# A hybrid mLSTM and GLA decoder step: three column tiles at the head of the weight stream, in nine small steps, with matmuls of ones ahead of the data

## The chip, the cores and the metric

The kernel runs on one core of one Trainium2 chip. The metric is the device time of one launch in microseconds. Each time below is the median of several runs; beside it stands one profiled execution, from which all rows are taken.

## The reference, cut to what matters

One layer takes 264 rows of activations (256 positions of a prompt, and 8 decode sequences of one position), projects them with one wide weight, runs two recurrent branches, merges them and ends with a LayerNorm:

```
p = x @ w_in                                   # (264, 2048) @ (2048, 13336)
qk_pre, a_v, a_i, a_f, a_o, a_z, b_q, ... = split(p)
qk = silu(causal_conv4(qk_pre))                # the first 2048 columns
...  mLSTM branch, GLA branch, headwise norms, gates ...
ya, yb = ya @ w_pa, yb @ w_pb
y = (sigmoid(g_a) * ya + sigmoid(g_b) * yb) @ w_out
out = layernorm(ALPHA * x + y)
```

All inputs are float32. Every weight is used once, for all 264 rows.

## The kernel before, in words

The kernel is a stream of column tiles ("units", the list of `units()`). A unit is 128 columns of a weight: 16 k tiles of 128 rows each. TensorE holds a weight tile of 128 x 128 and streams the 264 activation columns of one k tile past it. For float32 accuracy each operand is split in two: `hi` is the value rounded by ScalarE to the fast float32r format (`A.copy`), `lo` is the rest, which VectorE subtracts. A k tile then takes three matmuls into the same PSUM bank: hi·x_hi (line 224), hi·x_lo (line 225), lo·x_hi (line 228). A unit is thus 48 matmuls.

Weights come by DMA on SP's queue in pieces of up to 8 k tiles (`load_raw`, a ring of 4 raw buffers), `cast_piece` splits a piece (rings of 5 buffers each for hi and lo), and `group` runs the matmuls of a unit. The order of TensorE's instructions is the order in which the program is written (`manual_schedule`); the other engines' instructions are ordered by priority, casts of weights ahead. Each unit has an epilogue on ScalarE and VectorE; for the first 16 units it is `e_qk`, the convolution and SiLU, which reads the unit's PSUM bank. The pool `ps_m` holds three such banks, `ps_s` five for other work.

The head is special, since x is not in SBUF yet. The first HU = 2 units are loaded in pieces of KH = 4 k tiles, and go through together: for each of four steps the program loads four k tiles of x (line 1120, 528 KiB) and then four k tiles of unit 0 and of unit 1 (line 182, 256 KiB each, side by side in one raw buffer), splits x (lines 210 and 211), splits each unit's piece (lines 204 and 205), and runs the 12 matmuls of unit 0 and of unit 1 on these k tiles. After the four steps the unit loop (from line 1132) starts with the epilogues of units 0 and 1 and the stream of unit 2.

The parameters `par` and `cst`, which the convolution needs, are loaded behind the head's loads (lines 1130 and 1131).

Of the kernel before, what the change touches and what calls it, by code (L numbers as in the profile page):

```python
# [13 lines left out]
F32 = mybir.dt.float32  # L14
F32R = mybir.dt.float32r
# [8 lines left out]
T = L + NB  # L24
KT = 16
# [7 lines left out]
SMALL = 48  # L33
# [10 lines left out]
KR = 8  # L44
# [1 line left out]
CAST_BUFS = 5  # L46
NC = KT // KR
LA = CAST_BUFS - NC
HU = 2
KH = 4  # L50

COL = {}
_off = 0
# [28 lines left out]


@with_exitstack
def body(ctx, tc, xT, wbig, wsmall, par, cmask, lmask, rowc, gate, wgu, cT, sT, nst, cst, lnr,
         y, yd, pC, pn, pm, pconv, pS, sC, sn, sm, sS):
    nc = tc.nc
    V, A, G, PE = nc.vector, nc.scalar, nc.gpsimd, nc.tensor
    const = ctx.enter_context(tc.tile_pool(name="const", bufs=1))
    wraw_p = ctx.enter_context(tc.tile_pool(name="wraw", bufs=RAW_BUFS))  # L90
    whi_p = ctx.enter_context(tc.tile_pool(name="whi", bufs=CAST_BUFS))
    wlo_p = ctx.enter_context(tc.tile_pool(name="wlo", bufs=CAST_BUFS))
# [4 lines left out]
    ps_m = ctx.enter_context(tc.tile_pool(name="ps_m", bufs=3, space=PSUM))  # L97
    ps_s = ctx.enter_context(tc.tile_pool(name="ps_s", bufs=5, space=PSUM))
    UN = units()

    def t4(shape, name, dt=F32):
        return b4.tile(shape, dt, tag="b4", name=name)
# [37 lines left out]
    ones = const.tile([128, 128], F32, name="ones")  # L140
# [10 lines left out]
    x_hi = [const.tile([128, 4, T], F32R, name=f"xh{i}") for i in range(4)]  # L151
    x_lo = [const.tile([128, 4, T], F32R, name=f"xl{i}") for i in range(4)]
# [2 lines left out]
        return ap.bitcast(F32)  # L155


    pieces = [(u, k, KH, u) for k in range(0, KT, KH) for u in range(HU)]
    idx = HU
    for n, (kind, j) in enumerate(UN):  # L160
        if n < HU:
            continue
# [3 lines left out]
    last = {n: i for i, (n, k, w, bi) in enumerate(pieces)}  # L166
    raws, his, los = {}, {}, {}
    nxt = {"dma": 0, "cast": 0}

    def load_raw():  # L170

        i = nxt["dma"]
        if i >= len(pieces):
            return
        r = wraw_p.tile([128, KR, 128], F32, tag="raw", name="raw")
        o = 0
        while i < len(pieces) and o + pieces[i][2] <= KR:
            n, k, m, bi = pieces[i]
            w = 128 if bi is not None else SMALL
            src = wbig[bi] if bi is not None else wsmall  # L180
            raws[i] = r[:, o:o + m, 0:w]
            nc.sync.dma_start(out=raws[i], in_=src[:, k:k + m, :])
            o += m
            i += 1
        nxt["dma"] = i

    def cast_piece():
        i = nxt["cast"]
        while nxt["dma"] <= i:
            load_raw()  # L190
        n, k, m, bi = pieces[i]
        nxt["cast"] += 1
        r = raws.pop(i)
        h = whi_p.tile([128, KR, 128], F32R, tag="hi", name="hi")[:, 0:m]
        if bi is None:
            w = SMALL
            A.copy(out=h[:, :, 0:w], in_=r)
            V.tensor_tensor(out=h[:, :, w:2 * w], in0=r, in1=f(h[:, :, 0:w]), op=ALU.subtract)
            for q in range(m):
                his[n, k + q] = h[:, q, 0:2 * w]  # L200
            return
        lo = wlo_p.tile([128, KR, 128], F32R, tag="lo", name="lo")[:, 0:m]
        with tc.high_priority(offset=PRIO):
            A.copy(out=h, in_=r)  # L204
            V.tensor_tensor(out=lo, in0=r, in1=f(h), op=ALU.subtract)  # L205
        for q in range(m):
            his[n, k + q], los[n, k + q] = h[:, q], lo[:, q]

    def split(hi, lo, src):
        A.copy(out=hi, in_=src)  # L210
        V.tensor_tensor(out=lo, in0=src, in1=f(hi), op=ALU.subtract)

    def parts(n, k0, k1, rhs, base=0):

        small = UN[n][0] == "small"
        m = 2 * SMALL if small else 128
        ps = ps_m.tile([128, 512], F32, tag="mm", name="mm")
        out = ps[0:m, 0:T]
        for k in range(k0, k1):
            if k % KH == 0:  # L220
                yield ps[:, 0:T]
            wh = his[n, k]
            rh, rl = rhs(k - base)
            PE.matmul(out, lhsT=wh, rhs=rh, start=(k == k0), stop=False)  # L224
            PE.matmul(out, lhsT=wh, rhs=rl, start=False, stop=small and k == k1 - 1)  # L225
            if small:
                continue
            PE.matmul(out, lhsT=los[n, k], rhs=rh, start=False, stop=(k == k1 - 1))  # L228

    def group(*a, **kw):  # L230
        for ps in parts(*a, **kw):
            pass
        return ps

    def x_rhs(k):
        return x_hi[k // 4][:, k % 4, :], x_lo[k // 4][:, k % 4, :]
# [873 lines left out]

    with tc.manual_schedule(engines=MANUAL):
        V.memset(ones, 1.0)
        V.memset(inv256, 1.0 / 256.0)
        V.memset(eps_c, EPS)
        V.memset(one_c, 1.0)
        first = [parts(u, 0, 16, x_rhs) for u in range(HU)]
        head = {}
        for i in range(4):
            xr = t4([128, 4, T], "xr")
            nc.sync.dma_start(out=xr, in_=xT[:, 4 * i:4 * i + 4, :])  # L1120
            while nxt["dma"] < HU * (i + 1):
                load_raw()
            split(x_hi[i], x_lo[i], xr)
            for u in range(HU):
                cast_piece()
                head[u] = next(first[u])
        for u in range(HU):
            for _ in first[u]:
                pass
        nc.sync.dma_start(out=par_sb, in_=par)  # L1130
        nc.sync.dma_start(out=cst_sb, in_=cst)
        for n, (kind, j) in enumerate(UN):
            st['n'] = n
            while nxt["cast"] < min(last[n] + 1 + LA, len(pieces)):
                cast_piece()
                while nxt["dma"] < min(nxt["cast"] + RAW_BUFS - 1, len(pieces)):
                    load_raw()
            if kind == "pab":
                pa = group(n, 0, 8, lambda k: (st["yah"].t(k), st["yal"].t(k)))
                pb = group(n, 8, 16, lambda k: (st["ybh"].t(k), st["ybl"].t(k)), base=8)  # L1140
                e_pab(pa, pb, j)
            elif kind == "out":
                ln_pre(j)
                if j >= 8:
                    ln_shift(j)
                ps = group(n, 0, 16, lambda k: (mh.t(k), ml.t(k)))
                e_out(ps, j)
            else:
                ps = head[n] if n in head else group(n, 0, 16, x_rhs)
                if n == 0:  # L1150
                    g_conv_prep()
                if n == 4:
                    V.tensor_copy(out=im_sb, in_=ident)
                    for dst, src in ((gate_sb, gate), (wgu_sb, wgu), (rc_sb, rowc), (cm_sb, cmask), (lm_sb, lmask)):
                        nc.sync.dma_start(out=dst, in_=src)
                if kind == "qk":
                    for _ in e_qk(ps, j):
                        pass
                elif kind == "small":
                    add(g_gates(ps), True)  # L1160
                elif kind == "av":
                    e_v(ps, j, "avt", "avd")
                elif kind == "bv":
                    e_v(ps, j, "bvt", "bvd")
                elif kind == "bq":
                    e_plain(ps, j, "gq", Q_SCALE)
                elif kind == "bk":
                    e_plain(ps, j, "gk")
                elif kind in ("ao", "az"):
                    e_raw(ps, 2 * j + (kind == "az"), "ozr", 4, g_oz)  # L1170
                elif kind == "bz":
                    e_raw(ps, j, "bzr", 4, g_bz)
                elif kind in ("ga", "gb"):
                    e_raw(ps, 2 * j + (kind == "gb"), "gr", 4, g_g)
            pump(BUDGET)
            if kind == "gb" and j == 15:
                drain()
        ln_final()
# [18 lines left out]
def _layout(v):  # L1197
# [5 lines left out]
    d = {}  # L1203
# [1 line left out]
    d["xT"] = np.ascontiguousarray(x.T.reshape(16, 128, T).transpose(1, 0, 2))  # L1205
    w_in, w_pa, w_pb, w_out = v["w_in"][0], v["w_pa"][0], v["w_pb"][0], v["w_out"][0]
    un = units()
    big = np.empty((len(un) - 1, 128, 16, 128), w_in.dtype)
    i = 0
    for kind, j in un:  # L1210
        if kind == "small":
            continue
        if kind == "pab":
            c = slice(j * 128, j * 128 + 128)
            big[i, :, 0:8] = w_pa[:, c].reshape(8, 128, 128).transpose(1, 0, 2)
            big[i, :, 8:16] = w_pb[:, c].reshape(8, 128, 128).transpose(1, 0, 2)
        else:
            src, c0 = (w_out, j * 128) if kind == "out" else (w_in, COL[kind] + j * 128)
            big[i] = src[:, c0:c0 + 128].reshape(16, 128, 128).transpose(1, 0, 2)
        i += 1  # L1220
# [11 lines left out]
    lnr = np.zeros((128, D), np.float32)  # L1232
# [11 lines left out]
    for l in range(5):  # L1244
        hs = 1 << l
        j = np.arange(64)[None, :]
# [65 lines left out]
```

## Time and profile before

| | |
|---|---|
| time, median of 3 runs | 833.69 us (833.45 to 833.74) |
| the profiled execution, its own time | 835.32 us |
| its span, first to last instruction | 833.2 us |
| TensorE busy | 817.1 us, 98% of the span |
| VectorE, ScalarE busy | 593.2 us (71%), 444.8 us (53%) |
| DMA, mean over the span | 224 GB/s |
| mean granted TensorE clock | 0.997 |

Busy time of TensorE counts each matmul from its start to a modelled end, so that consecutive ones overlap; its idle time is more telling than its busy time. The time of an execution is some 2 us above its span, and the medians are read against each other.

### The profile page before, as it was taken

How to read it: one execution, taken by the hardware profiler on the slowest of the kernel's cores; microseconds unless marked ns; L12 is line 12 of the kernel's file. 1: busy time of each engine (PE TensorE's matmuls, PEld its weight loads, DVE VectorE, ACT ScalarE, POOL GpSimd, SP SyncE). 2: the span in 40 equal slices, each digit the busy share in tenths (PEclk: the TensorE clock that was granted, in tenths of full speed). 3: DMA queues.
4: the chain of work that ended last, by engine and by line, in shares of the span. 5: the costliest groups of instructions: out<-in, count | busy, mean ns of one | idle time of the engine just before them, and what ended most of it. 6: DMA issues, size and time to landing. Idle time of an engine off the chain costs nothing.

```text
span 833.2 us, 16677 instructions
## 1 busy us (share of the span) xinstructions
PE 817.1 (98%) x6750; PEld 807.6 (97%) x6750; DVE 593.2 (71%) x971; ACT 444.8 (53%) x669; POOL 44.4 (5%) x75
## 2 busy tenths in 40 slices
PE   6999999999999999999999999999999999999996
PEld 6999999999999999999999999999999999999995
DVE  6877667645567688867667997798746767667962
ACT  5755457545554465455546766566544444444633
POOL 0000000000000000001000000012000000000311
PEclk9999999999999999999999999999999999999998
DMA  8765564857658885688778588987555555576613
GB/s 323 249 199 182 152 205 155 234 181 253 236 185 303 299 298 197 214 281 296 262 253 313 192 284 330 301 277 230 187 183 184 184 179 179 181 252 203 188 39 105
DMA packets 55797, 186.30 MB, mean 224 GB/s; under 512 B 8340, under 2 KB 9304, under 8 KB 55720
## 3 DMA queue, kind: packets, MB, share of 16 engines
q1 hardware_dynamic: 51592, 170.82, 62.6%
q0 software_dynamic: 4128, 14.42, 4.5%
q8 instruction: 53, 0.87, 0.4%
q14 instruction: 24, 0.20, 0.1%
HBM read 168.50 MB, written 16.71 MB: 222 GB/s over the span
## 4 chain that ended last, share of the span: by engine, by line
PE 94%; DVE 2%; DMA 2%; issue 1%; ACT 0%; ACTq 0%; SPq 0%; POOLq 0%; POOL 0%; DVEq 0%
PE mm L224 29%; PE mm L225 29%; PE mm L228 29%; DMA gak<-rows_d 1%; DVE lo L205 1%; PE sd L464 1%; PE sd L702 1%; DMA raw<-wbig 1%; PE sd L423 1%; PE sd L404 0%; PE sd L438 0%; PE sd L753 0%; PE sd L996 0%; PE sd L312 0%; PE sd L964 0%
## 5 line engine op out<-in xcount | busy, mean ns | idle before, releaser
L224 PE MATMUL mm<-xh,hi 128*128 128x264 f32 x1552 | 445.9, 288 | 7.4 <-ACT hi L204 7.4
L225 PE MATMUL mm<-xl,hi 128*128 128x264 f32 x1552 | 440.1, 284 | 0.0
L228 PE MATMUL mm<-xh,lo 128*128 128x264 f32 x1536 | 435.9, 284 | 0.0
L204 ACT CAST hi<-raw 128x1024 fp32r<-128x1024 f32 (+1 forms) x260 | 268.1, 1034 | 274.1 <-PE mm L225 224.5
L205 DVE TENSOR_TENSOR lo<-raw,hi 128x1024 fp32r<-128x1024 f32 (+1 forms) x260 | 314.7, 1214 | 111.4 <-ACT hi L204 107.2
L224 PEld LDWEIGHTS mm<-xh,hi 128*128 128x128 f32 x1552 | 292.9, 189 | 9.0 <-ACT hi L204 7.4
L225 PEld LDWEIGHTS mm<-xl,hi 128*128 128x128 f32 x1552 | 293.1, 189 | 0.2
L228 PEld LDWEIGHTS mm<-xh,lo 128*128 128x128 f32 x1536 | 288.9, 188 | 0.2 <-DVE lo L205 0.2
L225 PE MATMUL mm<-ml,hi 128*128 128x264 f32 x256 | 72.9, 285 | 0.0
L224 PE MATMUL mm<-mh,hi 128*128 128x264 f32 x256 | 72.8, 285 | 0.0
L228 PE MATMUL mm<-mh,lo 128*128 128x264 f32 x256 | 72.5, 283 | 0.0
L566 DVE SCALAR_TENSOR_TENSOR cch<-kq,avd,cch 128x256 f32<-128x256 f32 x64 | 29.1, 480 | 37.0 <-DMA kq<-kq_d 37.0
L224 PEld LDWEIGHTS mm<-mh,hi 128*128 128x128 f32 x256 | 48.2, 188 | 0.0
L228 PEld LDWEIGHTS mm<-mh,lo 128*128 128x128 f32 x256 | 48.1, 188 | 0.0
L225 PEld LDWEIGHTS mm<-ml,hi 128*128 128x128 f32 x256 | 48.0, 188 | 0.0
L551 ACT ACTIVATE cch<-cch,decb 128x512 f32<-128x512 f32 x32 | 21.6, 718 | 39.4 <-DMA cch<-cT 39.4
L225 PE MATMUL mm<-ybl,hi 128*128 128x264 f32 x128 | 36.4, 284 | 0.0
L224 PE MATMUL mm<-ybh,hi 128*128 128x264 f32 x128 | 36.4, 284 | 0.0
L225 PE MATMUL mm<-yal,hi 128*128 128x264 f32 x128 | 36.3, 284 | 0.0
L228 PE MATMUL mm<-yah,lo 128*128 128x264 f32 x128 | 36.3, 284 | 0.0
L224 PE MATMUL mm<-yah,hi 128*128 128x264 f32 x128 | 36.2, 283 | 0.0
L228 PE MATMUL mm<-ybh,lo 128*128 128x264 f32 x128 | 36.2, 283 | 0.0
(314 smaller groups left out, 806.2 us busy)
## 6 DMA issues: line engine op xcount, KB each, us to landing
raw<-wbig SPq DMA_DIRECT2D x252, 512.0 KB, 4.8
cch<-cT SPq DMA_DIRECT2D x16, 512.0 KB, 6.9
kq<-kq_d SPq DMA_DIRECT2D x16, 512.0 KB, 8.2
sC<-cch POOLq DMA_DIRECT2D x16, 512.0 KB, 5.3
sch<-sT SPq DMA_DIRECT2D x8, 512.0 KB, 8.5
gak<-rows_d SPq DMA_DIRECT2D x8, 512.0 KB, 7.6
sS<-sch POOLq DMA_DIRECT2D x8, 512.0 KB, 6.0
xr<-xT SPq DMA_DIRECT2D x4, 528.0 KB, 6.6
```

The lines of the kernel that those rows point to most:

```text
L204: A.copy(out=h, in_=r)
L205: V.tensor_tensor(out=lo, in0=r, in1=f(h), op=ALU.subtract)
L224: PE.matmul(out, lhsT=wh, rhs=rh, start=(k == k0), stop=False)
L225: PE.matmul(out, lhsT=wh, rhs=rl, start=False, stop=small and k == k1 - 1)
L228: PE.matmul(out, lhsT=los[n, k], rhs=rh, start=False, stop=(k == k1 - 1))
L423: PE.matmul(S[:, o:o + n], lhsT=kT.t(2 * h + d)[:, s0:s0 + 128], rhs=qT.t(2 * h + d)[:, t0:t0 + n], start=(d == 0), stop=(d == 1))
L464: PE.matmul(CN[:, 0:VC], lhsT=kw[:, s, d * 128:d * 128 + 128], rhs=vt[h // 2][:, s, h % 2, :], start=(s == 0), stop=(s == 1))
L551: A.activation(out=chunks[i][:, b], in_=chunks[i][:, b], func=AF.Copy, scale=decb[:, h, b0 + b:b0 + b + 1])
L566: V.scalar_tensor_tensor(out=c[:, b, e], in0=r[:, 0, b], scalar=avd[:, j, b0 + b:b0 + b + 1], in1=c[:, b, e], op0=ALU.mult, op1=ALU.add)
L702: PE.matmul(pl[s0:s0 + m, 4 * hf + h, n0:n0 + w].rearrange("p (n s) -> p n s", s=hs), lhsT=K[:, h, hf * 128 + s0:hf * 128 + s0 + m], rhs=r ...
```

## The change

The head takes three units (HU = 3) instead of two, and nine steps of 1, 1, 2, 2, 2, 2, 2, 2 and 2 k tiles instead of four steps of 4. A step has one load of x (132 KiB for each k tile) and one load of the weights of all three units (192 KiB for each k tile) from a new input `whead`, in which the three units' columns stand side by side by k tile. It splits x in one pair of instructions and the weights of all units in one pair, without the raised priority of `cast_piece`, and then runs its matmuls, unit by unit. Unit 0's sums are in a bank of `ps_s`, those of units 1 and 2 in banks of `ps_m`. Ahead of the first step, TensorE runs eight float32 matmuls of the `ones` tile by itself, 128 columns each, into a further bank of `ps_s`, whose content nobody reads.

The raw, hi and lo buffers of the head come from the same rings as before, one of each for a step, of which 3 or 6 of 8 tiles are used. The stream then goes on with unit 3. `wbig` no longer holds the first three units; what is loaded, and the number of matmuls on data, stay the same in total.

```
-HU = 2
-KH = 4
+HU = 3
+HEAD = (1, 1, 2, 2, 2, 2, 2, 2, 2)
...
-    pieces = [(u, k, KH, u) for k in range(0, KT, KH) for u in range(HU)]
-    idx = HU
+    pieces = []
+    idx = 0
...
+    def products(out, n, k, rhs, start, stop, base=0):
 
         small = UN[n][0] == "small"
+        wh = his[n, k]
+        rh, rl = rhs(k - base)
+        PE.matmul(out, lhsT=wh, rhs=rh, start=start, stop=False)
+        PE.matmul(out, lhsT=wh, rhs=rl, start=False, stop=small and stop)
+        if not small:
+            PE.matmul(out, lhsT=los[n, k], rhs=rh, start=False, stop=stop)
...
         V.memset(ones, 1.0)
+        warm = side_ps()
+        head = [(side_ps() if u == 0 else ps_m.tile([128, 512], F32, tag="mm", name="mm"))[:, 0:T] for u in range(HU)]
...
-        first = [parts(u, 0, 16, x_rhs) for u in range(HU)]
-        head = {}
-        for i in range(4):
-            xr = t4([128, 4, T], "xr")
-            nc.sync.dma_start(out=xr, in_=xT[:, 4 * i:4 * i + 4, :])
-            while nxt["dma"] < HU * (i + 1):
-                load_raw()
-            split(x_hi[i], x_lo[i], xr)
+        for _ in range(8):
+            PE.matmul(warm[:, 0:128], lhsT=ones, rhs=ones, start=True, stop=True)
+        k0 = 0
+        for m in HEAD:
+            k1, i, o = k0 + m, k0 // 4, k0 % 4
+            xr = t4([128, m, T], "xr")
+            nc.sync.dma_start(out=xr, in_=xT[:, k0:k1, :])
+            wr, wh, wl = (p.tile([128, KR, 128], dt, tag=t, name=t)[:, 0:HU * m].rearrange("p (k u) c -> p k u c", u=HU)
+                          for p, dt, t in ((wraw_p, F32, "raw"), (whi_p, F32R, "hi"), (wlo_p, F32R, "lo")))
+            nc.sync.dma_start(out=wr, in_=whead[:, k0:k1])
+            split(x_hi[i][:, o:o + m], x_lo[i][:, o:o + m], xr)
+            split(wh, wl, wr)
             for u in range(HU):
-                cast_piece()
-                head[u] = next(first[u])
-        for u in range(HU):
-            for _ in first[u]:
-                pass
+                for k in range(k0, k1):
+                    his[u, k], los[u, k] = wh[:, k - k0, u], wl[:, k - k0, u]
+                    products(head[u], u, k, x_rhs, k == 0, k == KT - 1)
+            k0 = k1
...
-            while nxt["cast"] < min(last[n] + 1 + LA, len(pieces)):
+            while nxt["cast"] < min(last.get(n, -1) + 1 + LA, len(pieces)):
...
-                ps = head[n] if n in head else group(n, 0, 16, x_rhs)
+                ps = head[n] if n < HU else group(n, 0, 16, x_rhs)
```

`parts` and the old `group` become `products` and a `group` without the pauses at every fourth k tile.

## Rows read from the trace of the kernel before

**Rows 1.** The profile page, part 1: busy time and share of the engines.

```profile
PE 817.1 (98%) x6750; PEld 807.6 (97%) x6750; DVE 593.2 (71%) x971; ACT 444.8 (53%) x669; POOL 44.4 (5%) x75
```

**Rows 2.** Waits of TensorE, whole span: total us, times, longest.

```profile
PE mm L224 <- ACT hi L204: 7.4, 1, 7.4
PE sd L702 <- DVE gq L709: 1.0, 1, 1.0
PE sd L642 <- DVE ns L635: 0.5, 1, 0.5
```

**Rows 3.** Timeline from 0 us, all engines: start, length, instruction, idle before.

```profile
0.84 0.17 DVE L1112 MEMSET ones<- 128x128 f32 x1 [0.84 <-PEq L1301]
...
4.41 1.07 ACT L210 CAST xh<-xr 128x1056 fp32r<-128x1056 f32 x1 [2.39 <-DMA xr<-xT]
...
6.71 1.29 ACT L204 CAST hi<-raw 128x512 fp32r<-128x512 f32 x2 [1.22 <-DMA raw<-wbig]
...
7.38 0.59 PE L224 MATMUL mm<-xh,hi 128*128 128x264 f32 x1 [7.38 <-ACT hi L204]
...
8.70 1.07 ACT L210 CAST xh<-xr 128x1056 fp32r<-128x1056 f32 x1 [0.70 <-DMA xr<-xT]
...
11.80 0.42 PE L224 MATMUL mm<-xh,hi 128*128 128x264 f32 x1
...
12.02 0.35 PE L225 MATMUL mm<-xl,hi 128*128 128x264 f32 x1
...
12.20 0.28 PE L228 MATMUL mm<-xh,lo 128*128 128x264 f32 x1
```

**Rows 4.** Busy time by stretch; (x) counts starts; last columns clock, DMA share, GB/s.

```profile
0.00:3.23 3.23, 0.00 (x0) 0.00 (x0) 0.32 (x4) 1.28 (x1) 0.20 (x4) 1.00 0.41 101
0.00:3.78 3.78, 0.00 (x0) 0.00 (x0) 0.32 (x4) 1.28 (x1) 0.20 (x4) 1.00 0.49 145
...
4.00:6.50 2.50, 0.00 (x0) 0.00 (x0) 0.98 (x1) 1.07 (x1) 0.00 (x0) 1.00 0.92 232
6.50:12.00 5.50, 4.62 (x19) 4.39 (x20) 3.83 (x6) 3.96 (x6) 0.00 (x0) 1.00 1.03 400
0.00:12.20 12.20, 4.82 (x20) 4.59 (x21) 5.33 (x10) 6.52 (x8) 0.20 (x4) 1.00 0.84 285
...
12.20:112.20 100.00, 100.00 (x829) 99.94 (x828) 76.82 (x135) 55.52 (x92) 0.72 (x1) 1.00 0.66 216
```

**Rows 5.** Timeline of SP's queue, 0 to 12 us.

```profile
1.19 0.90 SPq L182 DMA_DIRECT2D raw<-wbig  x2
...
10.04 0.33 SPq L1131 DMA_DIRECT2D cst_sb<-cst  x1
11.46 0.33 SPq L182 DMA_DIRECT2D raw<-wbig  x1
```

**Rows 6.** Groups by line and shape, 0 to 45 us: busy us, mean ns.

```profile
L205 DVE TENSOR_TENSOR lo<-raw,hi 128x1024 fp32r<-128x1024 f32 x12 | 14.6, 1221 | 1.2 <-ACT hi L204 1.2
L204 ACT CAST hi<-raw 128x1024 fp32r<-128x1024 f32 x13 | 13.4, 1048 | 5.7 <-PE mm L225 2.7 <-DVE lo L205 1.6 <-DMA raw<-wbig 1.5
L205 DVE TENSOR_TENSOR lo<-raw,hi 128x512 fp32r<-128x512 f32 x8 | 5.2, 686 | 0.6 <-ACT hi L204 0.6
...
L204 ACT CAST hi<-raw 128x512 fp32r<-128x512 f32 x8 | 4.6, 616 | 1.3 <-DMA raw<-wbig 1.2
...
L261 DVE SCALAR_TENSOR_TENSOR cacc<-mm,par_sb,cacc 128x254 f32<-128x254 f32 x5 | 2.4, 481 | 0.0
...
L248 DVE TENSOR_TENSOR dtap<-dtap,ct 128x128 f32<-128x128 f32 x2 | 0.6, 288 | 0.0
```

**Rows 7.** The chain that ended last, 185 to 190 us: eight plain float32 matmuls.

```profile
186.19 1.74 PE sd L464 x8
```

**Rows 8.** Stretches behind the last matmul, columns as in rows 4.

```profile
825.94:827.90 1.96, 0.00 (x0) 0.00 (x0) 0.20 (x1) 1.25 (x3) 0.33 (x1) 1.00 1.04 291
827.90:829.00 1.10, 0.00 (x0) 0.00 (x0) 0.00 (x0) 0.00 (x0) 0.53 (x2) 0.51 1.08 333
```

More of the change, by code (lines that the diff above doesn't have):

```diff
@@ L84, in body @@
 @with_exitstack
-def body(ctx, tc, xT, wbig, wsmall, par, cmask, lmask, rowc, gate, wgu, cT, sT, nst, cst, lnr,
+def body(ctx, tc, xT, whead, wbig, wsmall, par, cmask, lmask, rowc, gate, wgu, cT, sT, nst, cst, lnr,
          y, yd, pC, pn, pm, pconv, pS, sC, sn, sm, sS):
@@ L211, in split, with group @@
         V.tensor_tensor(out=lo, in0=src, in1=f(hi), op=ALU.subtract)
-    def parts(n, k0, k1, rhs, base=0):
+    def products(out, n, k, rhs, start, stop, base=0):
         small = UN[n][0] == "small"
-        m = 2 * SMALL if small else 128
+        wh = his[n, k]
[4 more added lines that the diff above has]
+            PE.matmul(out, lhsT=los[n, k], rhs=rh, start=False, stop=stop)
+    def group(n, k0, k1, rhs, base=0):
         ps = ps_m.tile([128, 512], F32, tag="mm", name="mm")
-        out = ps[0:m, 0:T]
+        out = ps[0:2 * SMALL if UN[n][0] == "small" else 128, 0:T]
         for k in range(k0, k1):
[L220 to L231, printed above, removed]
-            pass
-        return ps
+            products(out, n, k, rhs, k == k0, k == k1 - 1, base)
+        return ps[:, 0:T]
     def x_rhs(k):
@@ L1115, in body @@
         V.memset(one_c, 1.0)
-        first = [parts(u, 0, 16, x_rhs) for u in range(HU)]
-        head = {}
-        for i in range(4):
-            xr = t4([128, 4, T], "xr")
-            nc.sync.dma_start(out=xr, in_=xT[:, 4 * i:4 * i + 4, :])
-            while nxt["dma"] < HU * (i + 1):
-                load_raw()
-            split(x_hi[i], x_lo[i], xr)
-            for u in range(HU):
-                cast_piece()
-                head[u] = next(first[u])
-        for u in range(HU):
-            for _ in first[u]:
-                pass
+        for _ in range(8):
[10 more added lines that the diff above has]
+            split(wh, wl, wr)
+            for u in range(HU):
+                for k in range(k0, k1):
+                    his[u, k], los[u, k] = wh[:, k - k0, u], wl[:, k - k0, u]
+                    products(head[u], u, k, x_rhs, k == 0, k == KT - 1)
+            k0 = k1
         nc.sync.dma_start(out=par_sb, in_=par)
@@ L1207, in _layout @@
     un = units()
-    big = np.empty((len(un) - 1, 128, 16, 128), w_in.dtype)
+    big = np.empty((len(un) - 1 - HU, 128, 16, 128), w_in.dtype)
+    d["whead"] = np.ascontiguousarray(w_in[:, COL["qk"]:COL["qk"] + HU * 128].reshape(16, 128, HU, 128).transpose(1, 0, 2, 3))
     i = 0
-    for kind, j in un:
+    for kind, j in un[HU:]:
         if kind == "small":
@@ L1302 @@
     args = []
-    for name in ("xT", "wbig", "wsmall", "par", "cmask", "lmask", "rowc", "gate", "wgu", "cT", "sT", "nst", "cst", "lnr"):
+    for name in ("xT", "whead", "wbig", "wsmall", "par", "cmask", "lmask", "rowc", "gate", "wgu", "cT", "sT", "nst", "cst", "lnr"):
         a = arrays[name]
```

## The prediction, made before the changed kernel ran

> **What bounds the kernel now.** I read the busy shares first. TensorE works 817.1 of the 833.2 us [rows 1], so 16.1 us of the span hold no matmul. The waits of TensorE say where they are: 7.4 us before the first matmul, and 1.5 us in two waits in the middle [rows 2]. The other 7.3 us lie behind the last matmul at 825.94 us [rows 8]; the change does not touch them. Between the first and the last matmul TensorE is the bound: 829 matmuls start in the 100 us from 12.20 us, 0.1206 us apart [rows 4]. A head that reaches this pace earlier moves everything behind it forward by as much, unless a new wait takes it back.
>
> The timeline of the start shows two losses. The first matmul is at 7.38 us, released by a cast which had waited for the first weights until 6.71 us [rows 3]. And the first matmuls are slow: those at 11.80 and 12.02 us still stand 0.22 us apart, and from 12.20 us the pace is 0.1206 us [rows 3, 4]. For 264 columns these are the clock's two levels, 1.2 and 2.4 GHz; the window view's clock column says 1.00 in both stretches, so here I trust the distances. The clock rose about 4.7 us after the first matmul, and by 12.20 us 20 matmuls had started [rows 4]. So I ask one thing of the change: when does its 21st matmul on data start, with the full pace behind it? Before, that was 12.20 us.
>
> **Landing times.** All head loads are in one queue, so I treat them as a line of KiB. x's first load (528 KiB) is seen at 4.41 us, the first weights (784 KiB in all) at 6.71 us [rows 3]. SP's 14th load goes out at 10.04 us and its 15th at 11.46 us, with its queue idle before them [rows 5]; these fit the landings of the sixth (2080 KiB) and the seventh (2608 KiB), and I read this as eight loads in flight. From 784 KiB at 6.71 us to 2608 KiB at 11.40 us the line is 389 KiB/us, and it gives 10.04 us for 2080 KiB, just what the row shows, and 8.73 us for the fourth load (1568 KiB), seen at 8.70 [rows 3]. Early on it is slower: 256 KiB took the 2.3 us from 4.41 to 6.71, and the DMA engines, though 92% busy, moved 232 GB/s, against 400 from 6.5 us on [rows 4].
>
> Now the new loads: 324 KiB a k tile, 132 of x and 192 of weights.
> - Step 0 (324 KiB in all): by 3.23 us the engines had moved 101 GB/s x 3.23 us = 326 kB, or 319 KiB; by 3.78 us 535 KiB, and 528 KiB were seen at 4.41, some 0.6 us later [rows 4, 3]. So step 0 lands at 3.9 us.
> - Step 1 (648 KiB): between 4.41 and 6.71 us by its share, 120 of 256 KiB: 5.5 us.
> - Step 2 (1296 KiB): 6.71 + 512 / 389 = 8.0 us. Each later step of two k tiles is 648 / 389 = 1.67 us later.
>
> **The splits.** From 512 and 1024 columns, ScalarE's cast is 0.18 us + 0.84 ns a column, VectorE's subtraction 0.15 us + 1.05 ns a column [rows 6]. A step of two k tiles has 768 columns of weights (0.83 and 0.95 us) and 528 of x (0.63 and 0.70); a step of one has 384 (0.51 and 0.55) and 264 (0.41 and 0.43). Hand-overs take some 0.05 us [rows 3].
>
> **The new head on TensorE.** Step 0: weights at 3.9, cast to 4.4, first matmul at 4.46; the lo part is there at 5.0, and the nine matmuls at 0.22 us end at 6.6. Step 1: landed 5.5, lo part ready at 6.6, nine matmuls to 8.6. Step 2: landed 8.0, cast to 8.9, its hi matmuls (19th and 20th) from 8.95; VectorE ends the lo part at 9.9, and the 21st matmul starts at 9.97 us. The clock: 4.7 us after a first matmul at 4.46 is 9.2 us, in time. From there a step is 18 matmuls, 18 x 0.1206 = 2.17 us, against 1.67 of loads, 1.46 of ScalarE and 1.65 of VectorE: TensorE is the slowest and the lead grows. The tightest is step 3: landed 9.7, lo part 11.6, wanted at 9.97 + 16 x 0.1206 = 11.9.
>
> The sum: 12.20 - 9.97 = 2.2 us earlier. The profiled execution would be 835.32 - 2.2 = 833.1 us, and the median of the runs, 1.6 us below that execution, 833.69 - 2.2 = 831.5 us.
>
> **The rest of the change, at nothing.** The eight matmuls of ones wait only for the memset (0.84 us, first on VectorE [rows 3]). Eight float32 matmuls of 257 columns take 1.74 us at the high clock [rows 7], so 0.11 us for 128 columns, about 0.2 us at the low one: 1.1 to 2.7 us, covered by the wait for step 0. At worst, if fewer columns save nothing, they end at 1.1 + 8 x 0.44 = 4.6 us, 0.15 us into step 0, which has slack. Whether they raise the clock the rows cannot show: if they count, it rises from about 1.1 + 4.7 = 5.8 us on, which gives nothing as long as step 2's weights bind.
>
> SP: 18 loads at about 0.45 us each [rows 5]; step 2's weights are the sixth, out by 3.1 us. With eight in flight the ninth waits for the first (about 3.2 us), the tenth also for raw buffer 0, free when step 0's lo part is done, 5.0 us; four steps are queued by then. `par` and `cst` move behind the 18th load and land at 6.71 + (5547 - 784) / 389 = 19.0 us; the first reader that matters is unit 0's epilogue at about 23.5 us. Unit 3's first piece lands 1.3 us behind them and is split by 22.6 us; TensorE wants it at 9.97 + 124 x 0.1206 = 24.9 us. That is 2.3 us of cover; beyond it each us costs one. Moving unit 2 into the head adds no matmul.
>
> **What the pages say.** By the Trainium skill, "DMA: Bandwidth & Descriptors" (Rules for kernel authors; Bandwidth), loads should be batched to 1 MiB or more, and its table has 138 GB/s for 64 KB against 341 for 1 MB. This speaks against loads of 132 KiB: at 138 GB/s, as an estimate from that page, the 648 KiB of the first two steps alone would take 4.8 us behind the first issue. The rows here disagree in part: loads of 256 and 528 KiB together ran at 400 GB/s once eight were in flight [rows 4].
>
> **Rivals.**
> - *Loads go by count, not by KiB.* Every load is 128 rows, and in the slow stretch the engines were 92% busy at half the bytes [rows 4], as if a row had a price of its own. By count, step 0's weights (second load) land at 6.71 us, step 1's (fourth) at 8.70, step 2's (sixth) at 10.04 [rows 3, 5]; the 21st matmul is at 11.98 us and 0.2 us are gained: 833.5. Then the change does not do what it says: its first matmul comes hardly earlier. Against it: the same short rows of weights fit the 389 KiB/us from 6.71 us on. In between lies 832.5.
> - *The slow stretch was its own.* If 389 KiB/us hold from 4.41 us, step 2 lands at 6.4 us. Then TensorE's own low-clock pace binds (steps 0 and 1 end at 8.6), the 21st is at 9.0, a gain of 3.2 us; if the matmuls of ones also raise the clock, step 2's lo part binds at 8.3, a gain of 3.9 us: 829.8.
> - *The clock stays low: slower than before.* Pieces that arrive one by one leave TensorE idle between steps. Each us at 1.2 GHz behind 9.97 us costs 1 - 0.1206 / 0.22 = 0.45 us. The gain is gone if the clock rises only at 9.97 + 2.2 / 0.45 = 14.9 us; later than that the kernel is slower, at 18.6 us by 1.7 us: 835.4. For it: after the last matmul the clock fell to 0.51 after 1.96 us of idle time [rows 8], and the pause between the ones and step 0 is about 1.8 us. Against it: my steps 0 and 1 run nearly without a gap, and in the kernel before a lone start was enough. The Trainium skill, "TensorE: Matmul & The Clock Gate" (Why this matters for your kernels), also wants sustained activity before the clock rises, and calls loops that wait for a DMA between matmuls cold; the rows agree in that the clock rose late and fell with idle time [rows 4, 8].
> - *Given back behind the head.* Three epilogues fall due at once. Unit 4 reuses unit 1's bank at 24.9 + 5.8 = 30.7 us. VectorE has by then, from 20 us, three splits (3.7 us), the preparation (seven instructions like that of line 248, 2.0 us) and two epilogues of some 2.0 us (three like that of line 261, two shorter): 29.7 us [rows 6]. If two more splits come first, TensorE waits 1.3 us and the gain is 0.9: 832.8.
>
> **How the numbers follow.** 0.2% (1.7 us) is about what a measurement of this kernel can tell from no change. Landing by KiB with the clock in time has 0.5; its own range is 830.9 to 832.3, and a fifth of it falls short of 832.0. Loads by count, or halfway there, 0.2; the quick start 0.12; the late clock 0.1, of which 0.04 slower by over 0.2%; given back 0.08, of which 0.03 slower. Faster: 0.4 + 0.12 = 0.52; slower 0.07; the rest, 0.41, within 0.2%. The range goes from the quick start to loads by count, 829.9 to 833.5.
>
> **What would show it.** The first matmul on data at about 4.5 us, the 21st at about 10.0, distances of 0.12 us from there, and unit 3 from about 24.9 us without a wait. Step 2's cast should begin at 8.0 us, released by its DMA. A cast at 10 us means loads by count; distances of 0.22 us after 10 us mean the clock. A wait of TensorE between 24 and 40 us means the gain was given back. The prediction is wrong if the middle of the stream shows new waits, for I took it to move as one piece.

## The result, and the profile after

The changed kernel took 841.69 us (median of 4, 840.76 to 844.2) against 833.72 us for the kernel before: ratio 1.0095, interval 1.0073 to 1.0117. It is 8 us slower, where 2.2 us faster was forecast. The profiled execution is the slowest of the four (844.2 us, span 842.4 us).

In this profile the head came out nearly as predicted. The timeline of TensorE, from the start, and ScalarE's cast of step 2's weights:

```profile
1.06 3.78 PE L1115 MATMUL sd<-ones 128*128 128x128 f32 x16 [1.06 <-DVE ones L1108]
4.49 0.57 PE L218 MATMUL sd<-xh,hi 128*128 128x264 f32 x1
...
8.93 0.28 PE L219 MATMUL sd<-xl,hi 128*128 128x264 f32 x1
9.70 0.39 PE L221 MATMUL sd<-xh,lo 128*128 128x264 f32 x1 [0.49 <-DVE lo L211]
```

```profile
7.82 0.83 ACT L210 CAST hi<-raw 128x768 fp32r<-128x768 f32 x1 [0.33 <-DMA raw<-whead]
```

The first matmul on data is at 4.49 us (predicted 4.46), the 21st at 9.70 (predicted 9.97), the distances behind it are 0.12 us, and unit 3 begins at 24.88 us (predicted 24.9; 27.23 before). Up to here the change gains 2.35 us. Then come the waits of TensorE over the whole span (total, times, longest), which answer to [rows 2]:

```profile
PE mm L218 <- ACT co L260: 5.8, 1, 5.8
PE sd L638 <- DVE ns L631: 2.1, 2, 1.4
PE sd L1115 <- DVE ones L1108: 1.1, 1, 1.1
PE sd L218 <- ACT hi L210: 0.9, 2, 0.7
PE mm L221 <- DVE lo L205: 0.6, 1, 0.6
PE sd L221 <- DVE lo L211: 0.5, 1, 0.5
```

Of the 7.4 us of waiting ahead of the first matmul before, some 2.5 are left (the third, fourth and sixth line); the matmuls of ones fill part of the rest. But there is one wait of 5.8 us that did not exist. The windows show where, and what it brings with it (columns as in [rows 4]):

```profile
24.88:30.84 5.96, 5.96 (x50) 5.75 (x48) 4.71 (x6) 4.73 (x7) 0.00 (x0) 1.00 0.74 238
30.84:36.68 5.84, 0.00 (x1) 0.00 (x1) 4.84 (x7) 3.01 (x6) 0.00 (x0) 0.91 0.74 232
36.68:42.35 5.67, 5.67 (x26) 5.67 (x27) 3.83 (x10) 1.96 (x6) 0.00 (x0) 0.50 0.73 234
```

Unit 3 runs at full pace to 30.84 us. Unit 4 then waits to 36.68 us; meanwhile the granted clock falls (0.91 in the mean), and in the 5.67 us after the wait it is 0.50, 1.2 GHz: 26 matmuls where the high clock gives 47. Against the kernel before, unit 3 starts 2.35 us earlier, unit 4 then loses 5.99 us by the wait, and unit 5 another 2.62 us by the clock (8.52 us from unit 4's start to unit 5's, against 5.90): -2.35 + 5.99 + 2.62 = 6.26 us late at unit 5, which starts at 45.20 us, before at 38.94.

Most of the rest is in the second line of the waits, on the norm of the mLSTM branch, which was 0.5 us before [rows 2]:

```profile
460.00:465.00 5.00, 3.67 (x24) 2.80 (x22) 5.00 (x8) 3.58 (x8) 0.00 (x0) 1.00 0.63 208
465.00:470.00 5.00, 4.26 (x20) 4.09 (x21) 5.00 (x10) 4.97 (x12) 0.53 (x1) 0.66 0.71 211
```

TensorE is idle for 2.1 us of these, and again the clock falls behind the waits (0.66). VectorE is busy in all 10 us: it is the bound here. The profiled execution ends 9.2 us later than the one before (842.4 against 833.2). It is 5.2 us late at the first matmul of this norm (461.94 us against 456.75; the kernel before has lost 1.0 us at line 702 by then, which this profile has not), so some 4 us of the 9.2 come from here on. The medians differ by 8.0, so this second loss is probably not as large in every execution. No run was made on its cause.

What held unit 4? The chain that ended last, followed back from its first matmul (start, length, what):

```profile
26.31 0.47 DVE cacc L257
26.78 1.14 DVE lo L205
...
27.94 5.69 DMA raw<-wbig
...
33.73 1.05 ACT hi L204
...
34.81 1.23 DVE lo L205
36.03 0.40 DVE cacc L257
...
36.46 0.18 ACT co L260
...
36.68 0.59 PE mm L218
```

Read it upwards. Unit 4's first matmul needs a PSUM bank; the last reader of unit 1's bank is the small copy `co` at 36.46 us. The copy waits for VectorE's third tap of unit 1's convolution (`cacc`), which stands in VectorE's queue behind the split of a later unit's weights (`lo`), which waits for its cast, which waits for a load issued at 27.94 us that took 5.69 us. So unit 1's epilogue stands in two queues behind splits of weights for later units. By the count of the casts in line 204, of which each unit takes two from 21.82 us on, these are units 5 and 6, and the last of them has no data yet. The ScalarE timeline says the same:

```profile
28.34 0.17 ACT L260 COPY co<-sd 128x11 f32<-128x11 f32 x1 [0.99 <-DVE cacc L257]
...
30.15 1.03 ACT L204 CAST hi<-raw 128x1024 fp32r<-128x1024 f32 x1
31.09 0.57 ACT L255 ACTIVATE cacc<-mm,par_sb 128x264 f32<-128x264 f32 x1
31.55 1.03 ACT L204 CAST hi<-raw 128x1024 fp32r<-128x1024 f32 x1
33.73 1.04 ACT L204 CAST hi<-raw 128x1024 fp32r<-128x1024 f32 x1 [1.15 <-DMA raw<-wbig]
36.46 0.17 ACT L260 COPY co<-mm 128x11 f32<-128x11 f32 x1 [1.69 <-DVE cacc L257]
```

And now the kernel before, the same copies of units 0, 1 and 2, and unit 4's first matmul:

```profile
24.49 0.17 ACT L264 COPY co<-mm 128x11 f32<-128x11 f32 x1 [0.92 <-DVE cacc L261]
...
32.82 0.17 ACT L264 COPY co<-mm 128x11 f32<-128x11 f32 x1 [0.39 <-DVE cacc L261]
...
33.04 0.39 PE L224 MATMUL mm<-xh,hi 128*128 128x264 f32 x1
...
35.80 0.17 ACT L264 COPY co<-mm 128x11 f32<-128x11 f32 x1 [0.94 <-DVE cacc L261]
```

There, too, unit 1's bank came free only at 32.99 us, 11.7 us after the head's last matmul began at 21.31, and unit 4 started at 33.04. The kernel before met that date by chance, since unit 2 was still to run behind its head. In the changed kernel the bank comes free at 36.64 us, 11.9 us after the head's last matmul began at 24.76, as before, but only unit 3 lies between the head and unit 4: it is wanted after 6 us.

### The profile page after: what moved, and what is told of

Read it like the earlier page. It is cut to its first block, busy times and chain, and to the rows that moved or that the text cites. A ratio compares the mean times of both kernels' runs of the same rounds, so it can differ in the third digit from the quotient of the medians.

```text
span 842.4 us, 16725 instructions
## 1 busy us (share of the span) xinstructions
PE 823.9 (98%) x6766; PEld 813.0 (97%) x6766; DVE 595.3 (71%) x975; ACT 445.2 (53%) x673; POOL 44.8 (5%) x75
## 4 chain that ended last, share of the span: by engine, by line
PE 87%; DMA 5%; DVE 5%; issue 2%; ACT 1%; SPq 1%; ACTq 0%; POOLq 0%; POOL 0%; DVEq 0%
PE mm L218 27%; PE mm L219 26%; PE mm L221 26%; DMA gak<-rows_d 3%; DVE lo L205 2%; PE sd L698 1%; PE sd L460 1%; DVE sch L804 1%; DMA raw<-wbig 1%; PE sd L419 1%; DMA raw<-whead 1%; DVE gpr L805 1%; PE sd L400 0%; PE sd L434 0%; PE sd L749 0%
## 5 line engine op out<-in xcount | busy, mean ns | idle before, releaser
L218 PE MATMUL mm<-xh,hi 128*128 128x264 f32 (+1 forms) x1536 | 442.3, 288 | 5.8 <-ACT co L260 5.8
L219 PE MATMUL mm<-xl,hi 128*128 128x264 f32 (+1 forms) x1536 | 436.4, 285 | 0.0
L204 ACT CAST hi<-raw 128x1024 fp32r<-128x1024 f32 x250 | 261.6, 1047 | 278.3 <-PE mm L219 234.0
L205 DVE TENSOR_TENSOR lo<-raw,hi 128x1024 fp32r<-128x1024 f32 x250 | 307.6, 1233 | 118.2 <-ACT hi L204 116.1
L218 PEld LDWEIGHTS mm<-xh,hi 128*128 128x128 f32 (+1 forms) x1536 | 290.8, 189 | 7.6 <-ACT co L260 6.0
L219 PEld LDWEIGHTS mm<-xl,hi 128*128 128x128 f32 (+1 forms) x1536 | 291.0, 189 | 0.3
L562 DVE SCALAR_TENSOR_TENSOR cch<-kq,avd,cch 128x256 f32<-128x256 f32 x64 | 29.2, 481 | 29.7 <-DMA kq<-kq_d 27.3
```

Source lines behind the costliest of these rows:

```text
L218: PE.matmul(out, lhsT=wh, rhs=rh, start=start, stop=False)
L562: V.scalar_tensor_tensor(out=c[:, b, e], in0=r[:, 0, b], scalar=avd[:, j, b0 + b:b0 + b + 1], in1=c[:, b, e], op0=ALU.mult, op1=ALU.add)
```

## The experiments

Each ran beside the kernel before on the same chip; ratios are to it. The first matmuls of the units, from the timelines of the profiled executions (us):

| | 21st on data | unit 3 | unit 4 | unit 5 | ratio (interval) |
|---|---|---|---|---|---|
| before | 12.20 | 27.23 | 33.04 | 38.94 | 1 |
| changed | 9.70 | 24.88 | 36.68 | 45.20 | 1.0095 (1.0073 to 1.0117) |
| banks | 10.69 | 25.88 | 31.68 | 37.48 | 0.9993 (0.9982 to 1.0004) |
| banks, no ones | 10.59 | 26.93 | 32.73 | 38.53 | 0.9983 (0.9970 to 0.9996) |
| two units | 8.91 | 28.11 | 33.91 | 39.71 | 1.0015 (1.0002 to 1.0028) |
| fill | 10.69 | 27.40 | 38.65 | 45.95 | 1.0057 (1.0037 to 1.0078) |
| copy out | 10.60 | 25.78 | 31.58 | 39.22 | 0.9997 (0.9979 to 1.0016) |
| banks, priority | 10.29 | 25.46 | 31.26 | 37.06 | 0.9983 (0.9974 to 0.9992) |
| even steps | 10.29 | 25.67 | 31.47 | 37.27 | 0.9984 (0.9973 to 0.9995) |
| before, with ones | 11.44 | 26.67 | 33.00 | 38.90 | 1.0008 (0.9996 to 1.0020) |
| best | 9.79 | 24.97 | 30.77 | 36.57 | 0.9966 (0.9954 to 0.9977) |
| even steps, eleven ones | 9.49 | 24.66 | 30.46 | 36.27 | 0.9976 (0.9962 to 0.9990) |

**The head's banks out of the way.**

```
-        head = [(side_ps() if u == 0 else ps_m.tile([128, 512], F32, tag="mm", name="mm"))[:, 0:T] for u in range(HU)]
+        head = [side_ps()[:, 0:T] for u in range(HU)]
```

> The sums of all three head units lie in banks of ps_s, so that units 3, 4 and 5 find the three banks of ps_m free; nothing else is changed. Theory (the bank): TensorE's 5.84 us wait before unit 4 at 30.8 us is for unit 1's bank alone, and the low clock from 36.7 to 42.3 us (some 2.5 us) follows from that idle time. Both go: 841.7 - 8.3 = 833.4 us, and 831 to 832 if the waits in the middle also become those of the kernel before. Rival (the backlog): VectorE and ScalarE are simply late behind a three-unit head, and the wait moves to the next thing that needs them, unit 6's bank or a split; then the time stays above 838 us.

834.06 us, 0.9993: the changed kernel's 8 us are gone. Its `co` copy of unit 1 is as late as ever, at 37.66 us, but nobody needs that bank, and unit 4 starts at 31.68 us without a wait. The wait did not move on, except for a little: unit 6 waits 0.5 us for unit 3's bank.

```profile
37.66 0.16 ACT L260 COPY co<-sd 128x11 f32<-128x11 f32 x1
```

```profile
PE sd L218 <- ACT hi L210: 2.0, 2, 1.2
PE sd L638 <- DVE ns L631: 1.2, 1, 1.2
PE sd L1115 <- DVE ones L1108: 1.1, 1, 1.1
PE mm L218 <- ACT co L260: 0.5, 1, 0.5
PE sd L221 <- DVE lo L211: 0.5, 1, 0.5
```

The first line is the head's price in this execution: step 2's weights came 1 us later than in the changed kernel's profile, so the 21st matmul is at 10.69 us.

**A copy that frees the bank.** The banks stay as in the changed kernel; the head units' epilogues read a copy of the sums.

```
+        if c < HU:
+            raw_sums = tmp.tile([128, T], F32, tag="t1", name="csum", bufs=T1_BUFS)
+            with tc.high_priority(offset=2 * PRIO):
+                A.copy(out=raw_sums, in_=ps)
+            ps = raw_sums
```

> The changed kernel with its banks as they are, but the epilogues of the three head units begin with one ScalarE copy of the sums to SBUF (0.57 us, raised priority) and read the copy: a unit's bank is free after that copy, and the rest of the epilogue stays as late as it is. Theory (the bank is held by the place of the epilogue in the queues of ScalarE and VectorE, not by the amount of work): unit 1's bank is free at about 30.7 us, TensorE waits for it under 1 us, the clock stays up: 833 to 835 us. Rival (the engines are so far behind that any reader of the sums comes late): a wait of 3 us or more before unit 4, above 837.5 us.

834.16 us, 0.9997, as expected. Unit 1's bank is free after a copy at 29.84 us, and unit 4 does not wait. Unit 2's copy is still behind a split, which itself waits for a buffer, and comes at 38.81 us, so unit 5 waits 1.7 us for it. The amount of work was not the cause: this kernel has three more instructions, and 8 us less.

```profile
29.84 0.36 ACT L256 COPY csum<-mm 128x264 f32<-128x264 f32 x1
...
37.53 1.04 ACT L204 CAST hi<-raw 128x1024 fp32r<-128x1024 f32 x1 [2.32 <-PE mm L219]
38.48 0.42 ACT L266 ACTIVATE csg<-cacc 128x264 f32<-128x264 f32 x1
38.81 0.36 ACT L256 COPY csum<-mm 128x264 f32<-128x264 f32 x1
```

**The wait filled with matmuls.**

```
+                if n == 4:
+                    fill = side_ps()
+                    for _ in range(12):
+                        PE.matmul(fill[:, 0:128], lhsT=ones, rhs=ones, start=True, stop=True)
                 ps = head[n] if n < HU else group(n, 0, 16, x_rhs)
```

> The changed kernel with twelve matmuls of ones (written to a spare bank) between units 3 and 4, in the wait. Theory: the wait for the bank stays, unit 4 starts at about 36.6 us as in the changed kernel, but TensorE's longest idle stretch is cut to some 3 us, the clock does not fall, and the 2.5 us of low clock are saved: 839.2 us. Rival (the low clock is not from this idle stretch, or costs nothing): 841.7 us, the clock falls again.

839.66 us, 1.0057: 0.4% below the changed kernel's ratio, about what was expected, but the two intervals just overlap. The reason given was only half right. The ones ran for 2.84 us, 2.6 us of idle time remained, and the clock fell all the same, as the rival had it:

```profile
33.20:36.00 2.80, 2.80 (x26) 2.65 (x24) 2.30 (x4) 2.33 (x4) 0.00 (x0) 1.00 0.69 247
36.00:38.00 2.00, 0.04 (x1) 0.00 (x0) 2.00 (x4) 0.62 (x1) 0.00 (x0) 1.00 0.75 242
38.00:41.50 3.50, 2.85 (x13) 2.85 (x14) 2.38 (x8) 1.49 (x6) 0.00 (x0) 0.54 0.77 226
```

But it was back up at about 41.5 us, 2.9 us after unit 4's start instead of 5.7: from unit 4's start to unit 5's are 7.30 us, against 8.52 in the changed kernel and 5.80 without a fall. So the wait's low clock is worth about 2.6 us, and the ones saved 1.2 of them in this profile. Unit 4 starts at 38.65 us, 2 us later than expected, and unit 3 begins at 27.40 us, for in this profile the clock fell in the head too: from 11.07 to 14.37 us the matmuls are 0.22 us apart.

**One part alone: the ones in the kernel before.**

```
         V.memset(ones, 1.0)
+        warm = side_ps()
+        for _ in range(8):
+            PE.matmul(warm[:, 0:128], lhsT=ones, rhs=ones, start=True, stop=True)
```

> The kernel before with one part of the change alone: the eight matmuls of ones ahead of the data. Theory: at the low clock they last from 1.1 to 4.8 us (0.22 us for each of 16 passes, as in the changed kernel), and the first data matmul comes at 7.4 us as before; in the pause of 2.6 us the clock may fall back, so the gain is between 0 and 20 x 0.1 = 2 us, and I expect 0.5 to 1.5 us, with some of the first 20 matmuls 0.12 us apart. Rival (the ones are worth nothing to matmuls that come after a pause): 17 distances of 0.22 us as before, and no gain within 0.2 us.

835.57 us, 1.0008: no gain, where 0.5 to 1.5 us were expected. Its timeline tells more than its time. The 21st matmul is 0.76 us earlier than before, unit 3 0.56 us, which need not be the ones' doing: in the last two kernels below, whose heads have no ones, the 21st matmul is at 11.90 and 11.71 us. Unit 4 starts at 33.00 us, as before (33.04), because it has to wait:

```profile
32.35 0.28 PE L228 MATMUL mm<-xh,lo 128*128 128x264 f32 x1
33.00 0.39 PE L224 MATMUL mm<-xh,hi 128*128 128x264 f32 x1 [0.37 <-ACT co L264]
```

In this profile, what is gained ahead of unit 4 is lost at unit 1's bank, even with a head of two units.

**The ones left out.** As the first experiment, without the eight matmuls of ones.

```
-        for _ in range(8):
-            PE.matmul(warm[:, 0:128], lhsT=ones, rhs=ones, start=True, stop=True)
```

> As e1_banks, and without the eight matmuls of ones. Theory: step 2's lo part decides when the full pace begins, and a clock that rises 4.7 us after the first matmul on data is in time; at most 0.5 us slower than e1_banks, the first matmul on data still at 4.5 us. Rival (the ones are needed): with pauses between the steps the clock rises only after 12 us; 1 to 3 us slower than e1_banks.

833.67 us, 0.9983, no slower than with them. The time is the theory's, but the clock is the rival's: without ones it rose only at about 13 us, 9 us after the first matmul on data at 4.15 us (22 distances of 0.22 us in the head, where a rise at 9.2 us had been assumed), and unit 3 began 1.05 us later than in the first experiment. Why this does not show in the time was not tested; the intervals of the two overlap, and the profile without ones has 0.3 us of waits at the later norm where the other has 1.2.

**Two units in nine steps.**

```
-HU = 3
+HU = 2
```

> HU = 2: the nine steps, the weights side by side and the matmuls of ones, but two units as before. Theory (the bank): unit 1's bank is wanted two units after the end of the head, as before; no wait at unit 4, and the shorter steps land earlier (260 KiB a k tile), so the head's gain of 2.5 to 3 us is kept: about 831 us. Rival (the small steps themselves delay what is behind the head, by loads, splits or their priority): 834 us or more.

835.98 us, 1.0015: the expectation was wrong. Unit 4 does not wait, as the theory has it, and the 21st matmul is at 8.91 us; but two waits behind the head take it back, for the split of unit 2's first piece:

```profile
PE mm L221 <- DVE lo L205: 1.2, 1, 1.2
...
PE mm L218 <- ACT hi L204: 0.9, 1, 0.9
```

The head's last matmul starts at 19.5 us, unit 2's first at 20.7, and unit 3 is 0.9 us later than before. The queues say why. ScalarE's cast of unit 2's first piece stands behind the first instruction of unit 0's epilogue, which waits for the last matmul of unit 0, and follows it without a wait for its load:

```profile
19.12 0.57 ACT L255 ACTIVATE cacc<-sd,par_sb 128x264 f32<-128x264 f32 x1 [1.86 <-PE sd L221]
19.59 1.03 ACT L204 CAST hi<-raw 128x1024 fp32r<-128x1024 f32 x1
```

VectorE's subtraction of the same piece starts at 21.16 us, behind three taps of that epilogue. So the time is the rival's, but of the causes that it lists the profile shows the order of splits and epilogues, not the loads. With three units no such wait shows.

**Priority for the head's epilogues, with the banks in `ps_s`.**

```
-                if kind == "qk":
+                if kind == "qk" and n < HU:
+                    with tc.high_priority(offset=2 * PRIO):
+                        for _ in e_qk(ps, j):
+                            pass
+                elif kind == "qk":
```

> As e1_banks (sums of the head in ps_s), and the epilogues of the three head units have a higher priority than the splits of weights, so that fewer splits stand ahead of them. Theory: e1_banks' last wait, 0.5 us of unit 6 for unit 3's bank at 43 us, goes, since the later epilogues move up; 0.3 to 0.8 us faster than e1_banks, clear of the kernel before by 0.1 to 0.2%. Rival (the splits then come late): TensorE waits for a cast or a lo part of unit 3 or 4, 1 us or more slower than e1_banks.

833.47 us, 0.9983, about as expected in time (its interval overlaps that of the first experiment), but not by the reason given: unit 6's wait for unit 3's bank is 1.0 us, not gone.

**Steps of two k tiles from the start.**

```
-HEAD = (1, 1, 2, 2, 2, 2, 2, 2, 2)
+HEAD = (2, 2, 2, 2, 2, 2, 2, 2)
```

> As e1_banks, with eight steps of two k tiles instead of 1, 1 and seven of 2. Theory: the full pace begins with the weights that complete 1296 KiB, and these land at the same time; the first matmul on data comes at about 6.2 us instead of 4.5, but the 21st within 0.5 us of e1_banks, and the time is that of e1_banks within 0.5 us. Rival (the single k tiles bring the gain): the 21st matmul and the time 1 to 1.7 us later than in e1_banks.

832.64 us, 0.9984: no slower than with the two single steps, and the 21st matmul at 10.29 us against 10.69, though the first on data comes 1.3 us later (5.80 us against 4.50). So the single steps do not bring the gain. Its profile is the slowest of its 12 executions (837.42 us). In it the clock fell in the head, with TensorE busy, behind a pause of 1.2 us between the ones and the first data:

```profile
4.60:5.80 1.20, 0.00 (x1) 0.00 (x1) 0.39 (x2) 0.83 (x1) 0.00 (x0) 1.00 0.97 304
5.80:7.50 1.70, 1.21 (x8) 1.00 (x9) 0.94 (x1) 0.63 (x1) 0.00 (x0) 1.00 1.04 338
7.50:10.90 3.40, 3.40 (x18) 3.40 (x17) 2.75 (x4) 2.70 (x4) 0.00 (x0) 0.51 1.02 396
```

```profile
8.77 0.96 DVE L211 TENSOR_TENSOR lo<-raw,hi 128x768 fp32r<-128x768 f32 x1 [0.56 <-ACT hi L210]
```

So here it is not the weights that complete 1296 KiB which set the 21st matmul, as the theory has it: their lo part was there at 9.73 us, and TensorE, at the low clock, came to it only at 10.29.

**No pause ahead of the data.** The next two lengthen the ones to eleven (`range(11)`), up to the first data: first with the raised priority, then without.

> e7_even_steps with the raised priority of e6_both and eleven matmuls of ones, which at the low clock last to about 5.9 us, when the first data are split. Theory: without a pause before the data the clock stays up through the head, the 21st matmul on data comes at 9.5 us or earlier, and the time is 0.5 us below e6_both and e7_even_steps, about 0.2 to 0.25% below the kernel before. Rival (the head is bound by its loads, the clock gives nothing): the time of e7_even_steps within 0.3 us.

> e7_even_steps with eleven matmuls of ones instead of eight and no raised priority: what of e9_best's lead over e7_even_steps (about 1.5 us) the longer ones bring. Theory: the clock stays at its high level through the head, since no pause stands between the ones and the data; 1 us or more below e7_even_steps, near e9_best. Rival (the order of the epilogues brought it): the time of e7_even_steps within 0.5 us, with distances of 0.22 us in the head again.

832.3 us, 0.9966 (0.9954 to 0.9977) with the priority, by the ratios 1.4 and 1.5 us below the two kernels that it combines, where 0.5 us was expected (the intervals just overlap). It is the only version whose interval lies wholly beyond 0.2%, and faster than both the kernel before and the changed one. Unit 3 starts at 24.97 us and unit 4 at 30.77 without a wait. Without the priority it is 833.09 us, 0.9976, 0.7 us below the even steps by the ratios, where 1 us or more was expected. In both profiles the clock was up by the fourth matmul on data, and stayed up (behind that one the only distances of 0.2 us or more are next to waits for a split), and unit 3 starts 0.7 to 1.0 us earlier than in the even steps with eight ones. The intervals of the two overlap, and that of 0.9976 meets the 0.9984 of eight ones, so the priority and the longer ones cannot be told apart by time. That the longer ones kept the clock up is not shown either: with eight ones and pauses of up to 1.2 us between the steps it stayed up through the head in the profiles of the first experiment and of the changed kernel, and fell in those of the even steps and of the fill.

**The reverse, which did not come about.** Two kernels were to give the kernel before the banks' order of the changed one, so that unit 3 would need unit 1's bank: unit 0's sums in `ps_s`, and a bank passed over before unit 3, unwritten in the first and written by one matmul of ones in the second.

```
+        if n == 3:
+            skip = ps_m.tile([128, 512], F32, tag="mm", name="mm")
+            PE.matmul(skip[:, 0:128], lhsT=ones, rhs=ones, start=True, stop=True)
-        ps = ps_m.tile([128, 512], F32, tag="mm", name="mm")
+        ps = side_ps() if n == 0 else ps_m.tile([128, 512], F32, tag="mm", name="mm")
```

> The kernel before, with unit 0's sums in a bank of ps_s and one bank of ps_m passed over once before unit 3, so that unit 3 (not unit 4) takes unit 1's bank: the banks' order of the changed kernel, with nothing of its head. Theory (the bank): unit 1's bank is free at 33.0 us as before, unit 3 wants it at 27.2; TensorE waits 5.8 us, the clock falls, and the time is 7 to 9 us above the kernel before, as in the changed kernel. Rival (the nine steps, their loads and splits make the loss): within 1 us of the kernel before.

> As e10_before_bank_skipped, where unit 3 did not wait: a bank that nothing writes was not passed over. Here one matmul of ones is written to it ahead of unit 3 (0.2 us), so that unit 3 takes unit 1's bank. Theory (the bank): unit 3 waits from 27.2 us until unit 1's epilogue lets go at about 33 us, the clock falls and costs some 2.5 us more, and the time is 7 to 9 us above the kernel before. Rival (the changed kernel's loss comes from its nine steps): within 1 us of the kernel before.

835.1 us (1.0002) and 835.0 us (1.0001), as the rivals had it, but neither made the condition: in the second, unit 3 waits 0.15 us for the matmul of ones itself, so it seems to have been given the same bank and not unit 1's.

```profile
26.73 0.38 PE L219 MATMUL mm<-ones 128*128 128x128 f32 x2
27.26 0.36 PE L227 MATMUL mm<-xh,hi 128*128 128x264 f32 x1 [0.15 <-PE mm L219]
```

They say nothing on the theory. The reverse test stays untried.

## Why the prediction was wrong

**Right, in part by luck: the head.** Landing by KiB held in the changed kernel's profile: step 2's cast began at 7.82 us (8.0 was forecast; step 1's at 6.20, where 5.5 was), the 21st matmul came at 9.70 and unit 3 at 24.88 us. The line of 389 KiB/us is no more than 1 us sure, though: in the other profiles with the same steps and three units the 21st came at 10.3 to 10.7 us, so that this close a match is luck. The clock was luck too. It was to rise 4.7 us after the first matmul on data, with or without the ones; without them it rose 9 us after it, at 13 us.

**Wrong: "moves everything behind it forward by as much".** This step of the prediction failed, for the stream behind the head does not hang on TensorE alone. Unit 1's bank comes free by the queues of ScalarE and VectorE and the loads of later units, and the step that priced this is the rival "given back behind the head". It added up VectorE's work (three splits, the preparation, two epilogues) to 29.7 us, 1.0 us before the bank is wanted at 30.7, and priced the wait at 1.3 us if two more splits come first. The bank came free at 36.64 us and the wait was 5.84 us. Two things were missing: the order in the queues, with epilogues behind splits that wait for loads, and the clock, which fell in the wait (2.6 us more). The mechanism was on the list, with a chance of 0.08 and a price of 1.3 us where 8.4 were due.

The trace of before had the warning. Not a sum of work was to be made, but one row read: the last reader of unit 1's bank, at 32.82 us, with the next user of that bank 0.05 us behind its end. A date that is just met can be a bound, though it shows as no wait at all in [rows 2]; here it was one, as the ones in the kernel before showed.

**Off, but covered: the ones.** They were put at 1.6 us, at worst 3.5; the worst came true (16 passes, 1.06 to 4.84 us). The reason is a misread row: the eight records of [rows 7] are not eight float32 matmuls but four, of two passes each (line 464 runs four of them for each head, 16 in all, and the trace has 32 records), so a pass was taken for a matmul. The ones brought the clock up at about 5 us. The prediction said that this gives nothing as long as step 2's weights bind; but in the one profile of three units without ones, where the clock rose later, unit 3 began 1.05 us later. The rival of the low clock had its place wrong in the changed kernel's profile: not between the steps, but behind the wait for the bank. In the fill's profile it came true in the head too.

**Not reached: the 2.2 us.** With the wait for unit 1's bank gone, the versions of three units with eight ones are at 0.9983 to 0.9997, 0.3 to 1.4 us below the kernel before and not 2.2. That lies inside the range of the prediction (829.9 to 833.5 us), which the changed kernel itself left by 8 us. Their profiles show where the rest can go, but no run separates it: the 21st matmul is later than forecast, so that unit 3 starts 1.3 to 1.8 us earlier than before; 0.2 to 1.7 us are lost again ahead of unit 5 or 6; and the waits at the norm of the mLSTM branch, where VectorE is busy throughout, are 0.6 to 2.0 us, against 0.5 before. A head's gain has this second place to be lost in, which the prediction did not look at.

## What to carry to other kernels

Before work is moved forward, list what the new position needs free, and read from the trace when each of these is really released: the last reader of a PSUM bank, not the sum of the work in front of it. A release and a next use that follow each other at once, without a wait, can mean that the two are in step and that a gain ahead of them stops there. When several groups are made to end together, their buffers are also wanted back sooner by as many groups; give them buffers of their own (here one line, and 8 us).

## What the runs showed of the chip that was not expected

The clock's fall did not follow one length of idle time. It fell after 1.96 us without a matmul behind the last one of the kernel before [rows 8], after about 2.2 us behind the ones of the fill (0.54 in the mean from 38.00 to 41.50 us), after about 4.8 us in the changed kernel's wait (a mean of 0.91 over 5.84 us), and in the profile with even steps while TensorE was busy, 1.7 us after it had taken up work again behind a pause of 1.2 us. In the first experiment's profile it did not fall behind a pause of 1.2 us. Once down, it stayed low for 3.0 to 5.8 us of steady matmuls in these profiles. A float32 matmul of 128 x 128 ones shows as two passes, of 0.22 us at the low clock and 0.11 at the high one.
